# Projections of a hybrid encoder layer as three fp32r products, with the q, k, v stream put first

## The chip, the cores and the metric

The kernel runs on one core of a Trainium2 chip, as one launch. The metric is the device time of that core in microseconds; lower is better. All work of the layer, from reading the inputs in device memory to writing the output there, is in this time.

## The reference

One encoder layer on a sequence of 512 tokens of width 1024 (batch 1), all in float32. The part around the change is the mixer at its start:

```python
h = _rmsnorm(x, norm_mix[l])
u, q, k, v, z, beta_f, beta_b, a_f, a_b = _split_cols(h @ w_in[l])   # w_in: 1024 x 2576
y_s5  = _s5_mixer(u, ...)          # forward and backward complex scan, 32 groups x 64 states
y_gdn = _gdn_mixer(q, k, v, z, beta_f, beta_b, a_f, a_b, ...)
#   depthwise conv of 5 taps + silu on q, k, v; l2norm of q and k;
#   gated delta rule in chunks of 64, forward and backward; times silu(z)
x = x + jnp.concatenate([y_s5, y_gdn], axis=-1) @ w_out[l]
x = x + _mem_xattn(_rmsnorm(x), _rmsnorm(mem), wq, wk, wv, wo)       # 256 memory tokens
x = x + _hier_moe(_rmsnorm(x), ...)                                   # 32 experts, top 2
return _rmsnorm(x, norm_final)
```

u, q, k, v and z are each 512 columns wide, the gates (beta and a, both directions) 16 columns together.

## The kernel before

**Engines and order.** The kernel is written on a layer that takes instructions in program order with a priority, simulates a time line when it is built, and fixes from it one order for each engine's queue. An engine then works through its queue strictly in order: an instruction that waits holds up all behind it. Where several streams are to run beside each other they are Python generators, and `weave` (L44) draws from them in a given proportion; instructions that are ready early can still be moved ahead of others that stand before them in the program.

**Stage one, projections (about 0 to 200 us).** `stage_a` (L154) loads x, normalises it (`rms_T`, L106) and leaves it transposed in the tile `ht` (128 partitions, 8 slices k, 512 tokens, float32): eight slices, TensorE transposes into PSUM, and alternately ScalarE and VectorE bring one slice with its gain back to SBUF (L128 to L131). `proj` (L179) makes 128 columns of `h @ w_in`: the weights come by `wcols` (L134, one DMA of 512 KB on SyncE's queue, tile `wst`, four buffers), and `mm8` (L140) runs eight float32 matmuls of 128x128 weights on 512 tokens. There are 20 such blocks: four of u (`proj_u`, L188), twelve of q, k and v (`gdn_in` and `gdn_conv`, L611 and L627), four of z (`proj_z`, L676). `gates` (L517) makes the 16 columns of the gates with matmuls at L539.

After a q, k or v block the convolution runs: ScalarE copies the block to `xp` (L636) and starts `cv` (L637), VectorE adds four taps (L639), ScalarE applies silu (L640), TensorE transposes (L648), q and k are normalised with a `pow` on GpSimd (L666) and transposed once more (L673). `xp` has two buffers, and its edges are cleared by GpSimd (L633, L634). Beside it runs `s5_params` (L232): a long chain of small VectorE operations, then eight rounds of complex products `cmul` (L221, six tensor products of 128x512 each, on VectorE or GpSimd by the tables at L54 and L55) that make `pm` and `ca`, transposes of `pm` (L372), `s5_u` (L396) and small matmuls (L381). `build` (L1510) weaves the twelve q, k, v blocks with this at L1559.

**Stage two, inverses (about 200 to 285 us).** `gdn_inv` (L685) builds and inverts the triangular blocks. Its tiles are allocated in a pool `gv` (L1563) that takes the place of the tiles of `s5_params`, so they wait until those are done. Beside it run `proj_z`, half of `mem_kv` (L945, keys and values of the memory, float32 matmuls of 256 tokens by the same `mm8`) and the first 16 steps of the recurrence `s5_rec` (L409, four short VectorE operations a step).

**Later stages.** `gdn_chain` (L789) with the rest of `mem_kv` and `s5_rec`, then `s5_out`, `s5_glu`, the mixer's output (`mix`, L920), cross attention and the experts, whose 96 MB of weights stream in as places for them come free. `mix`, `xattn` and `xattn_out` already use `mm3` (L145): a product of two float32 operands as three matmuls in the type fp32r, high times low, high times high and low times high, where the high half is the value copied to fp32r and the low half the rest. The weights of cross attention are split by `wsplit4` (L964): ScalarE copies the high half (L971), GpSimd subtracts (L972).

Of the kernel before, what the change touches and what calls it, by code (L numbers as in the profile page):

```python
# [9 lines left out]
F32 = mybir.dt.float32  # L10
F32R = mybir.dt.float32r
# [3 lines left out]
AF = mybir.ActivationFunctionType  # L15
OP = mybir.AluOpType
# [15 lines left out]
P = 128  # L32
T = 512
# [10 lines left out]
def weave(*streams):  # L44

    live = [[g, n, 0] for g, n in streams]
    while live:
        s = min(live, key=lambda t: (t[2] + 0.5) / t[1])
        s[2] += 1
        if next(s[0], s) is s:  # L50
            live.remove(s)


CA_ENG = (1, 1, 0, 1, 1, 1, 0, 1)  # L54
# [3 lines left out]
class Enc:  # L58
# [44 lines left out]
        return t  # L103


    def rms_T(self, pool, tiles, gain, out, tag, between=None, junk=None):  # L106

        nc = self.nc
        n = len(tiles)
        ss = pool.tile([P, 8], F32, name=tag + "ss", bufs=1)  # L110
        rs = pool.tile([P, 8], F32, name=tag + "rs", bufs=1)
        xn = []
        for i, t in enumerate(tiles):
            sq = junk if junk is not None else pool.tile([P, D], BF16, name=tag + "sq", bufs=1)
            nc.scalar.activation(sq, t, AF.Square, accum_out=ss[:, i:i + 1])
            nc.vector.tensor_scalar(ss[:, i:i + 1], ss[:, i:i + 1], 1.0 / D, 1e-6, op0=OP.mult, op1=OP.add)
            nc.gpsimd.tensor_tensor(rs[:, i:i + 1], ss[:, i:i + 1], self.nhalf[:, 0:1], op=OP.pow)
            nc.vector.tensor_scalar(t, t, rs[:, i:i + 1], None, op0=OP.mult)
            xn.append(t)
        if between:  # L120
            between()
        for k in range(8):
            ps = self.ps("tp")
            for i in range(n):
                nc.tensor.transpose(ps[:, i * P:(i + 1) * P],
                                    xn[i].rearrange("t (p k) -> t k p", k=8)[:, k, :], self.ident)
            src = ps[:, :n * P]
            if k % 2:  # L128
                nc.vector.tensor_scalar(out[:, k, :], src, gain[:, k:k + 1], None, op0=OP.mult)
            else:  # L130
                nc.scalar.activation(out[:, k, :], src, AF.Copy, scale=gain[:, k:k + 1])  # L131
        return xn

    def wcols(self, src, w):  # L134

        t = self.wp.tile([P, 8, w], F32, name="wst", bufs=4)
        self.nc.sync.dma_start(t, src)
        return t

    def mm8(self, ps, w, act):  # L140

# [12 lines left out]
    def stage_a(self):  # L154
        nc, tc, A = self.nc, self.tc, self.A
        pool = self.pa
        gain = self.col8('norm_mix', self.cp)
        x2d = A['x'][0]
        xt = []
        with tc.tile_pool(name="xp", bufs=1) as xp:  # L160
            for i in range(4):
                t = xp.tile([P, D], F32, name=f"x{i}")
                nc.sync.dma_start(t, x2d[i * P:(i + 1) * P, :])
                xt.append(t)
            self.ht = pool.tile([P, 8, T], F32, name="ht")
            self.pre = {}

            def first_weights():
                for c0 in (0, P):
                    self.pre[c0] = self.wcols(self.w_in(c0, P), P)  # L170
                self.w_g = self.wp.tile([P, 8, 16], F32, name="wg", bufs=1)
                nc.sync.dma_start(self.w_g, self.w_in(2560, 16))

            self.rms_T(xp, xt, gain, self.ht, "h", first_weights)

    def w_in(self, c0, w):
        return self.A['w_in'][0].rearrange("(p k) n -> p k n", k=8)[:, :, c0:c0 + w]

    def proj(self, c0):  # L179

        w = self.pre.pop(c0, None)
        if w is None:
            w = self.wcols(self.w_in(c0, P), P)
        ps = self.ps("mm")
        self.mm8(ps, w, self.ht)
        return ps

    def proj_u(self):  # L188
# [328 lines left out]
    def gates(self):  # L517
        nc, A, tc = self.nc, self.A, self.tc
# [5 lines left out]
        with tc.tile_pool(name="gt_", bufs=1) as tp:  # L524
# [6 lines left out]
            ps = self.ps("s5")  # L531
# [2 lines left out]
            sel = tp.tile([P, 16], F32, name="gsel")  # L534
            v.tensor_reduce(sel, self.ident.rearrange("p (i c) -> p c i", i=4)[:, :16], axis=AX.X, op=OP.add)
            for j in range(2):
                for i in range(4):
                    k = j * 4 + i
                    nc.tensor.matmul(ps[i * 32:i * 32 + 16], self.w_g[:, k], self.ht[:, k], start=(j == 0), stop=(j == 1))  # L539
            for i in range(4):  # L540
                nc.scalar.activation(gT[i * 32:i * 32 + 16], ps[i * 32:i * 32 + 16], AF.Copy)
            pt = self.ps("tp")
# [4 lines left out]
            y, ab, e, w, t1 = (tp.tile([P, 4, 8], F32, name="s" + n) for n in "yaewt")  # L547
# [128 lines left out]
    def proj_z(self):  # L676
        nc = self.nc
        for h in range(4):
            ps = self.proj(2048 + h * P)
            z = self.wp.tile([P, T], F32, name="zt", tag="ut", bufs=1)  # L680
            nc.scalar.activation(z, ps, AF.Silu)
            nc.sync.dma_start(self.z_scr[:, h], z)
            yield
# [826 lines left out]
    def build(self):  # L1510
# [41 lines left out]
        with tc.tile_pool(name="gi", bufs=2) as gi:  # L1552
            qkv = self.gdn_in([(w, n, h) for h in range(4) for w, n in ((1, "k"), (0, "q"))] +
                              [(2, "v", h) for h in range(4)], gi)
            s5 = self.s5_params()
            next(s5)
            for _ in u:
                pass
            weave((qkv, 13), (s5, 9))  # L1559

        self.gp2 = pool(left, "gp2")
        self.gp3 = pool(left, "gp3")
# [204 lines left out]
```

## Time and profile before

Three runs took 903.43, 900.66 and 902.88 us (median 902.88). The profile comes from one more execution, which took 903.52 us; its span, from the first to the last instruction, is 901.8 us, so that 1.7 us lie around it.

| what | value |
|---|---|
| TensorE (PE) busy | 790.2 us, 88% of the span, 4735 matmul records |
| TensorE weight loads (PEld) busy | 498.2 us, 55% |
| VectorE (DVE) busy | 406.2 us, 45% |
| ScalarE (ACT) busy | 328.4 us, 36% |
| GpSimd (POOL) busy | 233.9 us, 26% |
| DMA | 185.17 MB, mean 205 GB/s |
| mean granted TensorE clock | 0.942 |

How to read it: a row names the line of the kernel, the engine, the operation, the tile written and the tiles read, shapes, the count, and busy time. A float32 matmul of 512 columns shows as two records of TensorE, an fp32r matmul as one. A busy TensorE need not be at its peak, since matmuls are pipelined and their ends modelled. "Idle before" is time in which the engine waited ahead of these instructions, with the engine or transfer that ended the wait; PEclk is the clock that TensorE was granted, as a share of full speed. Time stamps are microseconds from the span's start.

### The profile page before, as it was taken

The page shows a single profiled execution, that of the slowest core. Times are in us where ns is not written, and L with a number is a line of the kernel's source. Part 1 is how long each engine was busy: PE and PEld are TensorE (multiplying, and loading weights), DVE is VectorE, ACT ScalarE, POOL GpSimd, SP SyncE. Part 2 cuts the span into 40 slices and gives each one's busy share as a digit, 9 for nine tenths or more (in the row PEclk, how much of TensorE's full clock was granted, in tenths as well). Part 3 has the DMA queues.
Part 4 walks back from the last instruction along what each step waited for, and adds up shares of the span by engine and source line. Part 5 has one row for each costly group of instructions (what it writes and reads, how often), then busy time and mean ns, then how long its engine had stood idle before and what let it go on. Part 6 is the DMA issues. An engine that isn't in the chain of part 4 may idle for free. (4 is left out here: it accounts for less than half of the span.)

```text
span 901.8 us, 13009 instructions
## 1 busy us (share of the span) xinstructions
PE 790.2 (88%) x4735; PEld 498.2 (55%) x4736; DVE 406.2 (45%) x1049; ACT 328.4 (36%) x758; POOL 233.9 (26%) x239
## 2 busy tenths in 40 slices
PE   5987998998997997899899999993988888788883
PEld 3444554555686876667688889992333333333331
DVE  4288667878898432245543544216000000000284
ACT  4333444454413355454334554431412221212214
POOL 1032776633100122115161322324111010101203
PEclk9997998999996998999999999996889999999997
DMA  8836222315562337516655324983899999999942
GB/s 208 150 87 100 89 64 73 121 53 187 179 189 60 107 64 175 101 43 205 206 179 182 123 71 164 328 325 123 316 413 413 412 414 412 400 399 407 391 186 95
DMA packets 128130, 185.17 MB, mean 205 GB/s; under 512 B 38734, under 2 KB 93006, under 8 KB 123968
## 3 DMA queue, kind: packets, MB, share of 16 engines
q1 hardware_dynamic: 122736, 172.31, 56.7%
q0 software_dynamic: 5328, 12.01, 3.5%
q8 instruction: 38, 0.62, 0.3%
q14 instruction: 28, 0.23, 0.1%
HBM read 165.50 MB, written 26.18 MB: 213 GB/s over the span
## 5 line engine op out<-in xcount | busy, mean ns | idle before, releaser
L143 PE MATMUL bank<-ht,wst 128*128 128x512 f32 x320 | 152.8, 626 | 2.6 <-ACT kd L583 2.4
L143 PEld LDWEIGHTS bank<-ht,wst 128*128 128x128 f32 x320 | 60.8, 199 | 71.9 <-issue 68.1
L1342 PE MATMUL bank<-mw,xt 128*64 128x512 f32 x320 | 87.7, 607 | 4.1 <-DVE yd L1386 3.3
L1383 PE MATMUL bank<-mw,hT 128*64 128x512 f32 x168 | 54.0, 710 | 19.1 <-ACT hT L1377 19.1
L143 PE MATMUL bank<-mt,wst 128*128 128x256 f32 x256 | 59.7, 392 | 0.0
L1342 PEld LDWEIGHTS bank<-mw,xt 128*64 128x64 f32 x320 | 31.6, 140 | 50.6 <-issue 40.4
L639 DVE SCALAR_TENSOR_TENSOR cv<-xp,taps,cv 128x512 f32<-128x512 f32 x48 | 50.4, 1049 | 20.3 <-ACT cv L637 19.3
L972 POOL TENSOR_TENSOR wlo<-wst,whi 128x1024 fp32r<-128x1024 f32 x16 | 38.6, 2414 | 78.8 <-ACT whi L971 78.8
L1346 DVE SCALAR_TENSOR_TENSOR hs<-hs,tw,bank 128x256 f32<-128x256 f32 x16 | 7.7, 480 | 113.8 <-ACT hs L1345 113.8
L1345 ACT ACTIVATE hs<-bank,tw 128x256 f32<-128x256 f32 x16 | 7.6, 475 | 139.6 <-PE bank L1342 139.6
L143 PEld LDWEIGHTS bank<-mt,wst 128*128 128x128 f32 x256 | 49.9, 198 | 7.7 <-issue 0.8
L1322 POOL DMA_INDIRECT xg<-t_scr,tidx x16 | 16.5, 1033 | 143.8 <-PE bank L1375 128.7
L1386 DVE COPY yd<-bank 128x512 f32<-128x512 f32 x13 | 9.0, 692 | 87.2 <-PE bank L1383 87.2
L824 POOL TENSOR_TENSOR kt<-kn,kd 64x512 f32<-64x512 f32 x14 | 14.5, 1035 | 97.6 <-PE bank L778 51.4
L1383 PEld LDWEIGHTS bank<-mw,hT 128*64 128x64 f32 x168 | 14.8, 158 | 44.3 <-issue 23.3
L1332 ACT ACTIVATE xt<-bank,gm 128x128 f32<-128x128 f32 x128 | 34.8, 383 | 10.2 <-PE bank L1329 10.0
L149 PE MATMUL bank<-wlo,oh 128*128 128x256 f32 x128 | 36.6, 289 | 0.0
L854 DVE SCALAR_TENSOR_TENSOR S<-S,egl,bank 128x128 f32<-128x128 f32 x48 | 15.5, 346 | 46.2 <-PE bank L851 46.2
L150 PE MATMUL bank<-whi,oh 128*128 128x256 f32 x128 | 35.8, 282 | 0.0
L151 PE MATMUL bank<-whi,ol 128*128 128x256 f32 x128 | 35.2, 287 | 0.0
L1342 PE MATMUL bank<-xh,xt 128*64 128x512 f32 x72 | 32.4, 593 | 0.8 <-DVE yd L1386 0.8
L149 PE MATMUL bank<-mlo,mxh 128*128 128x512 f32 x64 | 25.6, 403 | 0.3 <-DVE gss L484 0.3
(556 smaller groups left out, 1853.0 us busy)
## 6 DMA issues: line engine op xcount, KB each, us to landing
mw<-in_moe_w_down_dram SPq DMA_DIRECT2D x25, 1024.0 KB, 13.1
mw<-in_moe_w_gate_dram SPq DMA_DIRECT2D x40, 512.0 KB, 13.7
mw<-in_moe_w_up_dram SPq DMA_DIRECT2D x40, 512.0 KB, 13.3
wst<-in_w_in_dram SPq DMA_DIRECT2D x20, 512.0 KB, 4.5
xh<-in_moe_w_gate_dram SPq DMA_DIRECT2D x9, 512.0 KB, 12.6
xh<-in_moe_w_up_dram SPq DMA_DIRECT2D x9, 512.0 KB, 11.4
ca_scr<-ca SPq DMA_DIRECT2D x8, 512.0 KB, 2.8
wst<-in_xa_wk_dram SPq DMA_DIRECT2D x8, 512.0 KB, 4.5
```

Of the source, the lines that this page charges most:

```text
L143: self.nc.tensor.matmul(ps, w[:, k, :], act[:, k, :], start=(k == 0), stop=(k == 7))
L149: self.nc.tensor.matmul(ps, ah, bl, start=(first and i == 0), stop=False)
L150: self.nc.tensor.matmul(ps, ah, bh, start=False, stop=False)
L151: self.nc.tensor.matmul(ps, al, bh, start=False, stop=(last and i == n - 1))
L639: v.scalar_tensor_tensor(cv, xp[:, w:w + T], taps[:, w, m:m + 1], cv, op0=OP.mult, op1=OP.add)
L824: nc.gpsimd.tensor_tensor(kt[s], self.kn[s, ch // 2], self.kd[s, ch // 2, di * 4:di * 4 + 4, None].to_broadcast([64, 4, P]), op=OP.mult)
L854: v.scalar_tensor_tensor(sn, S[di, h], self.egl[:, ch % 2, ch // 2, di * 4 + h:di * 4 + h + 1], p, op0=OP.mult, op1=OP.add)
L972: nc.gpsimd.tensor_tensor(lo, st, hi.bitcast(F32), op=OP.subtract)
L1322: self.gather = g_.indirect_dma_start(out=xg, out_offset=None, in_=self.t_scr, in_offset=bass.IndirectOffsetOnAxis(ap=self.tidx[:, q:q + 1 ...
L1332: nc.scalar.activation(xt[:, k], ps[:, (k % 4) * P:(k % 4 + 1) * P], AF.Copy, scale=self.gm[:, k:k + 1])
L1342: nc.tensor.matmul(pg[w * 64:w * 64 + 64].rearrange("p (a n) -> p a n", a=2), xt[:, k, w * 64:w * 64 + 64], un[k // 4 * 2 + w][:, :, k % 4 ...
L1383: nc.tensor.matmul(py[w * 64:w * 64 + 64], hT[:, k, w * 64:w * 64 + 64], wd[w][:, k, c], start=(k == 0), stop=(k == 1))
```

## The change

The 20 projection blocks are no longer float32 matmuls but sums of three fp32r products. `ht` becomes two tiles, `hth` and `htl`; `rms_T` with `lo` given writes each slice twice, the high half by ScalarE from PSUM and the low half by VectorE from PSUM. `wsplit` loads a block's weights as before (`wst` has three buffers now), lets ScalarE copy the high half to `whi` and another engine subtract the low half into `wlo` (two buffers each): GpSimd for the first two u blocks and the four z blocks, VectorE for the other two u blocks and the twelve of q, k and v. `proj` calls `mm3` with eight slices: 24 matmuls instead of eight. The gates stay float32 and run twice, on the low and on the high half of h. The stream of the q, k, v blocks is wrapped in `ahead`, which issues all its instructions at high priority, so that the order made at build time prefers them (their loads and splits too) to those of `s5_params` beside them.

```diff
--- before.py
+++ after.py
@@ -49,6 +49,15 @@
         s[2] += 1
         if next(s[0], s) is s:
             live.remove(s)
+
+
+def ahead(tc, g):
+
+    while True:
+        with tc.high_priority():
+            if next(g, g) is g:
+                return
+        yield
 
 
 CA_ENG = (1, 1, 0, 1, 1, 1, 0, 1)
@@ -103,7 +112,7 @@
         return t
 
 
-    def rms_T(self, pool, tiles, gain, out, tag, between=None, junk=None):
+    def rms_T(self, pool, tiles, gain, out, tag, between=None, junk=None, lo=None):
 
         nc = self.nc
         n = len(tiles)
@@ -125,7 +134,11 @@
                 nc.tensor.transpose(ps[:, i * P:(i + 1) * P],
                                     xn[i].rearrange("t (p k) -> t k p", k=8)[:, k, :], self.ident)
             src = ps[:, :n * P]
-            if k % 2:
+            if lo is not None:
+                nc.scalar.activation(out[:, k, :], src, AF.Copy, scale=gain[:, k:k + 1])
+                nc.vector.scalar_tensor_tensor(lo[:, k, :], src, gain[:, k:k + 1], out[:, k, :].bitcast(F32),
+                                               op0=OP.mult, op1=OP.subtract)
+            elif k % 2:
                 nc.vector.tensor_scalar(out[:, k, :], src, gain[:, k:k + 1], None, op0=OP.mult)
             else:
                 nc.scalar.activation(out[:, k, :], src, AF.Copy, scale=gain[:, k:k + 1])
@@ -133,9 +146,18 @@
 
     def wcols(self, src, w):
 
-        t = self.wp.tile([P, 8, w], F32, name="wst", bufs=4)
+        t = self.wp.tile([P, 8, w], F32, name="wst", bufs=3)
         self.nc.sync.dma_start(t, src)
         return t
+
+    def wsplit(self, src, w, lo_eng):
+
+        st = self.wcols(src, w)
+        hi = self.wp.tile([P, 8, w], F32R, name="whi", bufs=2)
+        lo = self.wp.tile([P, 8, w], F32R, name="wlo", bufs=2)
+        self.nc.scalar.activation(hi, st, AF.Copy)
+        lo_eng.tensor_tensor(lo, st, hi.bitcast(F32), op=OP.subtract)
+        return hi, lo
 
     def mm8(self, ps, w, act):
 
@@ -162,27 +184,26 @@
                 t = xp.tile([P, D], F32, name=f"x{i}")
                 nc.sync.dma_start(t, x2d[i * P:(i + 1) * P, :])
                 xt.append(t)
-            self.ht = pool.tile([P, 8, T], F32, name="ht")
+            self.hth = pool.tile([P, 8, T], F32R, name="hth")
+            self.htl = pool.tile([P, 8, T], F32R, name="htl")
             self.pre = {}
 
             def first_weights():
                 for c0 in (0, P):
-                    self.pre[c0] = self.wcols(self.w_in(c0, P), P)
+                    self.pre[c0] = self.wsplit(self.w_in(c0, P), P, nc.gpsimd)
                 self.w_g = self.wp.tile([P, 8, 16], F32, name="wg", bufs=1)
                 nc.sync.dma_start(self.w_g, self.w_in(2560, 16))
 
-            self.rms_T(xp, xt, gain, self.ht, "h", first_weights)
+            self.rms_T(xp, xt, gain, self.hth, "h", first_weights, lo=self.htl)
 
     def w_in(self, c0, w):
         return self.A['w_in'][0].rearrange("(p k) n -> p k n", k=8)[:, :, c0:c0 + w]
 
-    def proj(self, c0):
-
-        w = self.pre.pop(c0, None)
-        if w is None:
-            w = self.wcols(self.w_in(c0, P), P)
+    def proj(self, c0, lo_eng=None):
+
+        hi, lo = self.pre.pop(c0, None) or self.wsplit(self.w_in(c0, P), P, lo_eng or self.nc.vector)
         ps = self.ps("mm")
-        self.mm8(ps, w, self.ht)
+        self.mm3(ps, [((hi[:, k, :], lo[:, k, :]), (self.hth[:, k, :], self.htl[:, k, :])) for k in range(8)])
         return ps
 
     def proj_u(self):
@@ -534,9 +555,11 @@
             sel = tp.tile([P, 16], F32, name="gsel")
             v.tensor_reduce(sel, self.ident.rearrange("p (i c) -> p c i", i=4)[:, :16], axis=AX.X, op=OP.add)
             for j in range(2):
-                for i in range(4):
-                    k = j * 4 + i
-                    nc.tensor.matmul(ps[i * 32:i * 32 + 16], self.w_g[:, k], self.ht[:, k], start=(j == 0), stop=(j == 1))
+                for part in (self.htl, self.hth):
+                    for i in range(4):
+                        k = j * 4 + i
+                        nc.tensor.matmul(ps[i * 32:i * 32 + 16], self.w_g[:, k], part[:, k].bitcast(F32),
+                                         start=(j == 0 and part is self.htl), stop=(j == 1 and part is self.hth))
             for i in range(4):
                 nc.scalar.activation(gT[i * 32:i * 32 + 16], ps[i * 32:i * 32 + 16], AF.Copy)
             pt = self.ps("tp")
@@ -676,7 +699,7 @@
     def proj_z(self):
         nc = self.nc
         for h in range(4):
-            ps = self.proj(2048 + h * P)
+            ps = self.proj(2048 + h * P, nc.gpsimd)
             z = self.wp.tile([P, T], F32, name="zt", tag="ut", bufs=1)
             nc.scalar.activation(z, ps, AF.Silu)
             nc.sync.dma_start(self.z_scr[:, h], z)
@@ -1556,7 +1579,7 @@
             next(s5)
             for _ in u:
                 pass
-            weave((qkv, 13), (s5, 9))
+            weave((ahead(tc, qkv), 13), (s5, 9))
 
         self.gp2 = pool(left, "gp2")
         self.gp3 = pool(left, "gp3")
```

## The prediction

> **What bounds the kernel now.** I read the page first, then a table of all engines by stage, the matmuls of L143 by stage, the waits of the second stretch, and the time line around single operations.
>
> ```profile
> PE 790.2 (88%) x4735; PEld 498.2 (55%) x4736; DVE 406.2 (45%) x1049; ACT 328.4 (36%) x758; POOL 233.9 (26%) x239
> ```
>
> 88% is a mean over unlike stages, so it says little. The table by stage (TensorE, weight loads, VectorE, ScalarE, GpSimd, then granted clock, DMA share, GB/s):
>
> ```profile
> 0.00:60.00 60.00, 49.53 (x163) 24.77 (x164) 29.82 (x141) 24.61 (x44) 6.48 (x15) 1.00 0.70 156
> 60.00:200.00 140.00, 127.12 (x834) 67.53 (x835) 103.79 (x150) 61.68 (x173) 82.68 (x86) 0.93 0.34 85
> 200.00:245.00 45.00, 42.54 (x345) 25.03 (x344) 39.02 (x147) 21.75 (x27) 10.38 (x6) 0.96 0.49 169
> 245.00:285.00 40.00, 34.06 (x251) 30.41 (x250) 39.41 (x173) 9.20 (x19) 0.00 (x0) 0.91 0.52 154
> 590.00:902.00 312.00, 245.83 (x1208) 114.51 (x1207) 68.53 (x160) 77.23 (x226) 54.77 (x60) 0.91 0.85 335
> ```
>
> The change works in the first three rows. From 60 to 200 us TensorE is busy 127 of 140 us, but VectorE is busy 104 and GpSimd 83: no engine has much room. From 200 to 285 us VectorE is the full one (78 of 85 us). The experts at the end move 335 GB/s, and their loads go out as places for them come free, so time saved ahead of them should reach the end whole.
>
> How much of this is the projections (the same stages, L143 alone: TensorE, weight loads):
>
> ```profile
> 0.00:60.00 60.00, 37.59 (x80) 15.10 (x80) 1.00 0.70 156
> 60.00:200.00 140.00, 86.44 (x176) 33.89 (x176) 0.93 0.34 85
> ```
>
> A block is 16 records, so five blocks lie before 60 us and eleven between 60 and 200; the four of z follow. What VectorE, GpSimd and TensorE wait for in that second stretch:
>
> ```profile
> POOL xp L633 <- DVE cv L639: 21.4, 7, 6.4
> DVE cv L639 <- ACT cv L637: 19.3, 8, 4.2
> ...
> PE bank L372 <- DVE pm L228: 5.7, 1, 5.7
> ```
>
> The convolution waits 19.3 us for ScalarE's copy, which waits for the projection. GpSimd stands 21.4 us before its clearing of `xp`, because the convolution still holds that buffer. This is a ring through TensorE, ScalarE, VectorE and GpSimd; TensorE is its longest part, VectorE the next.
>
> **The change part by part.** *TensorE.* Twenty float32 records in a row and the instruction behind them; two fp32r matmuls of 512 columns, 29 steps apart; the gates:
>
> ```profile
> 125.80 8.85 PE L143 MATMUL bank<-ht,wst 128*128 128x512 f32 x20
> 134.58 1.03 PE L404 MATMUL bank<-uperm,bct 128*64 128x64 f32 x28
> ...
> 465.37 0.39 PE L149 MATMUL bank<-mlo,mxh 128*128 128x512 f32 x1
> ...
> 471.94 0.39 PE L149 MATMUL bank<-mlo,mxh 128*128 128x512 f32 x1
> ...
> 28.03 1.91 PE L539 MATMUL bank<-ht,wg 128*16 128x512 f32 x16
> ```
>
> A float32 record takes (134.58 − 125.80)/20 = 0.439 us, a block of 16 records 7.0 us. An fp32r matmul takes (471.94 − 465.37)/29 = 0.227 us, a block of 24 takes 5.4 us. A block saves 1.6 us of TensorE: 8 us in the first five, 17.5 in the eleven, 6.4 in z, 32 in all. The gates run twice: +1.9. So TensorE loses 30 us of work, and that is the ceiling of the gain.
>
> *What comes in elsewhere.* Attention does the same operations already: ScalarE's high half of 128x1024, VectorE's low half of it, the pair that brings a slice from PSUM, and GpSimd's low half (least, median and greatest ns):
>
> ```profile
> L1001 ACT ACTIVATE kvh<-kvs x4: 1050/1060/1063, 496.4 to 506.2; 128x1024 fp32r<-128x1024 f32 x4
> L1002 DVE TENSOR_TENSOR kvl<-kvs,kvh x4: 1208/1224/2592, 497.5 to 507.3; 128x1024 fp32r<-128x1024 f32 x4
> L985 ACT ACTIVATE xh<-bank,c_norm_xattn x8: 682/691/703, 474.2 to 489.4; 128x512 fp32r<-128x512 f32 x8
> L986 DVE SCALAR_TENSOR_TENSOR xl<-bank,c_norm_xattn,xh x8: 742/743/751, 474.9 to 490.4; 128x512 fp32r<-128x512 f32 x8
> L972 POOL TENSOR_TENSOR wlo<-wst,whi x16: 2378/2398/2665, 463.9 to 596.7; 128x1024 fp32r<-128x1024 f32 x16
> ```
>
> Twenty high halves are 20 x 1.06 = 21 us of ScalarE, 12 of them between 60 and 200 us. It is busy 108 of the first 245 us, so they lie beside other work; without that room each would add its 1.06 us to a block. Fourteen low halves go to VectorE, at 1.21 us alone and 2.59 at worst, and six to GpSimd at 2.40. The slices cost four more operations of 0.69 us on ScalarE and four more of 0.74 on VectorE.
>
> *Why 2.59.* VectorE and GpSimd hold each other up. Here are four taps of a convolution beside GpSimd's products, two taps without them, and a product of the recurrence of 64 columns that meets one GpSimd operation, with the mean of its like:
>
> ```profile
> 123.22 5.45 DVE L639 SCALAR_TENSOR_TENSOR cv<-xp,taps,cv 128x512 f32<-128x512 f32 x4 [3.42 <-ACT cv L637]
> 75.17 1.53 DVE L639 SCALAR_TENSOR_TENSOR cv<-xp,taps,cv 128x512 f32<-128x512 f32 x2
> 222.43 1.26 DVE L414 TENSOR_TENSOR rt<-a8r,U 128x64 f32<-128x64 f32 x1
> 222.35 1.26 POOL L725 TENSOR_TENSOR qkd<-qkd,mk 128x512 f32<-128x512 f32 x1 [4.24 <-DVE qkd L724]
> L416 DVE TENSOR_TENSOR rt<-rt,rt 128x64 f32<-128x64 f32 x49 | 10.9, 222 | 0.8
> ```
>
> A tap takes 0.77 us alone and 1.36 in company, and the short product takes 1.26 us instead of 0.22 and ends just behind GpSimd's. The Trainium skill ("SBUF — State Buffer", section "SBUF: two separate sides") says that GpSimd and a VectorE operation with two SBUF inputs take one shared port pair in turns, each for its whole instruction. The trace agrees in these rows. By that rule alone, every low half would add its whole time to the other engine's queue, and the time would come out as in the rival "lock" below.
>
> *The second stretch, 60 to 200 us.* TensorE falls from 127.1 to 109.6 us. VectorE takes in eleven low halves; between 1.21 and 2.59 I take the middle, 1.9, since GpSimd is busy in 83 of the 140 us: +21, so 125 us. VectorE becomes the fullest engine, and it has waits of its own. The fullest engine now runs at 127/140 = 91%; at 93 to 95% for VectorE the stretch takes 131 to 134 us. I take a gain of 7. With 1.21 us a half VectorE has 117 us and at 93% the stretch takes 126: gain 14. With 2.59 it has 132 us, at 93% 142: loss of 2.
>
> *Priority.* The q, k, v stream now passes the products of `s5_params` on VectorE and GpSimd, and their stores on SyncE's queue: its loads, splits, taps and clearings go first. TensorE's wait of 5.7 us for `pm` goes, as the first convolution no longer stands behind those products and projections fill the hole. But `s5_params` ends later, and the inverses wait for its tiles. Today both end together; these are its last small matmuls and the first of the inverses:
>
> ```profile
> 195.94 0.66 PE L381 MATMUL bank<-ca,bb 64*32 64x128 f32 x16
> ...
> 200.60 0.68 PE L703 MATMUL bank<-lef,g 128*64 128x64 f32 x16
> ```
>
> I bound this by the size of that hole both ways, −6 to +6, and take −2, as z and the memory's keys can fill TensorE during a tail of `s5_params`.
>
> *The first 60 us.* TensorE alone doesn't set this stage:
>
> ```profile
> ACT ut L194 <- DMA u_scr<-ut: 6.2, 1, 6.2
> ...
> DVE fq L214 <- ACT ft L213: 6.4, 1, 6.4
> ```
>
> ScalarE waits 6.2 us with the second u block for the store of the first (`ut` has one buffer), and everything behind it on ScalarE waits too, so the chain of `s5_params` on VectorE stands 6.4 us. A quicker TensorE starts the store sooner but doesn't shorten it. At best the five blocks give 8; at worst the first block waits for its two halves (1.06 + 2.40) and the gates' 1.9 come on top, some 5 lost. I take a gain of 3.
>
> *After 200 us.* z gives TensorE 6.4 us, but VectorE is the full engine. GpSimd's four low halves can stop VectorE for 2.40 each: 0 to +9.6. In return the memory's blocks start sooner, and one of them stands between two matmul groups of the inverse:
>
> ```profile
> 278.78 6.82 PE L768 MATMUL bank<-XT,N 32*32 32x32 f32 x128 [5.94 <-issue]
> ...
> 286.01 6.22 PE L143 MATMUL bank<-mt,wst 128*128 128x256 f32 x16
> ```
>
> Moved into the hole of 5.94 us ahead, it gives up to 6. So −6 to +10; I take −1, since the recurrence, which fills much of VectorE here, can partly wait.
>
> *The sum.* −7 − 2 − 3 − 1 = −13 against the profiled execution's 903.5 us: 890.5. The median of the runs shown is 0.6 under that execution, so 890.
>
> **The rivals.** *Lock* (slower). VectorE and GpSimd become one resource. The second stretch loses 2, the four halves of z stop the inverses for 9.6, the first stage gives its 3: +8.6, so 911 us. For it: 1.36 against 0.77 us a tap. Against: GpSimd idles 57 of 140 us there, and z's halves may be made before the inverses begin. It decides once VectorE's mean low half is above 2.2 us.
>
> *Tail* (no change). q, k and v finish sooner, but `s5_params`, now behind them, ends at 200 us as before, since its work on GpSimd isn't less; the inverses start when they did. The first stage's 3 are lost in it, and some 3 remain from after 200 us: 900 us. For it: both streams end together today. Against: 21.4 us of GpSimd's waits hang on the convolution and shrink with it. If the priority alters no order at all, only its 2 us are missing.
>
> *Through* (much faster). TensorE's ring is the true bound everywhere, and all 30 us come through: 873 us. For it: 91% busy, and VectorE's largest wait (19.3 us) hangs on a projection. Against: VectorE's load above. The Trainium skill ("TensorE: Matmul & The Clock Gate", Part 1) adds that idle windows halve the clock, which a less filled TensorE would meet more often; by it this rival would end some us higher.
>
> **How the numbers follow.** Forecast 0.45, *through* 0.20, *lock* 0.20, *tail* 0.15. The forecast's own range is 878 to 902. To leave no more than 2 in 10 out, the range reaches from *through* to near *lock*: 873 to 909. A measurement of this kernel can tell about 0.3% (2.7 us) from no change. Faster by more than that: 0.43 of the forecast, all of *through*, a third of *tail*: 0.68. Within it: half of *tail* and the edges: 0.11. Slower: *lock* and the rest: 0.21.
>
> **What would show it.** In the profile after, L150 and its neighbours should show 24 records a block, 0.227 us apart; the low halves on VectorE a mean near 1.9 us; the first L703 near 188 us instead of 200.60; VectorE fuller than TensorE up to there. The forecast is wrong if L703 starts at 200 us or later, if the low halves come near 2.6 us, or if TensorE still is the fullest and the inverses start before 180 us.

## The result and the profile after

The changed kernel takes 899.07 us (median of 20 runs, 887.6 to 904.05); the kernel before takes 901.69 beside it (20 runs, 899.17 to 905.27). The ratio of the compared runs is 0.9931, with a 95% interval of 0.9910 to 0.9951: about 6 us faster. The comparisons here leave out runs more than 1.5% above the fastest of their kernel: five of these twenty (the other fifteen have a median of 896.31 us), two of the six of split_ut2_tz2 below, which stood near 1117 us at a granted clock of 0.64, and one of the kernel before at 2643 us. By the medians of all twenty runs on each side the change is only 2.6 us faster, so its worth is 3 to 6 us by the way of counting. The profiled execution of the changed kernel took 900.03 us, its span 898.2.

The first lines of the page, the table by stage (columns as before) and the matmuls that open the inverses, all of the changed kernel:

```profile
PE 779.6 (87%) x4911; PEld 539.8 (60%) x4912; DVE 434.9 (48%) x1067; ACT 348.6 (39%) x781; POOL 256.6 (29%) x245
```

```profile
0.00:60.00 60.00, 45.48 (x215) 33.80 (x217) 33.66 (x151) 34.61 (x59) 10.19 (x17) 0.94 0.71 157
60.00:200.00 140.00, 121.73 (x1009) 92.92 (x1008) 124.66 (x161) 73.01 (x182) 98.06 (x88) 0.93 0.38 93
200.00:245.00 45.00, 37.75 (x325) 31.06 (x325) 41.74 (x131) 21.32 (x28) 14.35 (x8) 0.96 0.46 161
245.00:285.00 40.00, 37.16 (x379) 32.67 (x378) 34.71 (x155) 12.03 (x24) 1.20 (x2) 0.91 0.44 127
```

```profile
L726 PE MATMUL bank<-lef,g x64: 222/222/270, 193.8 to 221.5; 128*64 128x64 f32 x64
```

TensorE's busy time fell by 10.6 us in all, not by 30. VectorE is now the fullest engine from 60 to 200 us, with the 125 us that were forecast. The inverses open at 193.8 instead of 200.60 us, where the prediction had 188. The waits of that stretch, one row of the kernel before that the prediction doesn't show, then those of the changed kernel:

```profile
ACT cv L640 <- DVE cv L639: 46.0, 10, 8.7
```

```profile
ACT cv L663 <- DVE cv L662: 25.0, 6, 8.0
POOL xp L656 <- DVE cv L662: 18.4, 6, 6.6
...
PE bank L393 <- DVE pm L249: 3.8, 2, 3.0
...
DVE cv L662 <- ACT cv L660: 1.9, 3, 1.1
```

Before, VectorE's taps waited 19.3 us for ScalarE's copy of a projection. Now they wait 1.9: the projections are ready when VectorE comes to them. ScalarE's wait for the taps is no sign of this, as it went down too, from 46.0 to 25.0 us.

The recurrent chain of the delta rule opens with the first `vn`. In the kernel before, then in the changed one (the two times are the first and the last start):

```profile
L841 ACT ACTIVATE vn<-bank,csv x32: 338/367/379, 300.4 to 415.9; 128x128 f32<-128x128 f32 x32
```

```profile
L864 ACT ACTIVATE vn<-bank,csv x32: 362/368/380, 284.9 to 405.3; 128x128 f32<-128x128 f32 x32
```

At 285 us the change is 15.5 us ahead, more than the whole forecast. At the last addition of the S5 half to the residual (481.4 instead of 482.8 us) 1.4 are left. What lies between is seen in the table for 340 to 412 us of the changed kernel:

```profile
340.00:364.00 24.00, 21.83 (x192) 16.40 (x190) 6.96 (x21) 15.31 (x27) 4.93 (x12) 0.93 0.71 138
364.00:388.00 24.00, 23.78 (x124) 18.15 (x124) 5.88 (x13) 4.67 (x10) 0.43 (x4) 0.51 0.07 26
388.00:412.00 24.00, 23.61 (x198) 18.09 (x196) 11.83 (x25) 12.10 (x27) 3.08 (x8) 1.00 0.32 104
```

TensorE looks full in the middle row, but its granted clock is 0.51, and it gets 124 matmuls done where the next row has 198. Ahead of this stands one gap, in the time line of TensorE:

```profile
362.09 0.38 PE L825 MATMUL bank<-vn,qkd 64*64 64x128 f32 x2
364.22 0.66 PE L467 MATMUL bank<-tz,uperm 128*64 128x128 f32 x2 [1.75 <-issue]
```

L467 is the first product of the second half of `s5_out`, and it needs the second load of `tz`. That tile has one buffer, so SyncE issues the load's eight pieces once the first half's products are done, and each takes 7.2 us to land (time line of SyncE, then the view of the tile):

```profile
353.29 3.76 SPq L451 DMA_DIRECT2D tz<-w_scr  x8
```

```profile
DMA to landing us min/median/max: 7.0/7.2/7.4
```

The last piece is issued at 356.6 and lands near 363.8 us; TensorE starts at 364.22. The row names no transfer ("issue"), so that this load is the cause is shown only by the run below that takes the wait away. The runs' own clocks say the same: at a mean granted clock of 0.941 the changed kernel took 889.07 us, at 0.928 it took 897.14 to 900.03, and at 0.924 it took 900.16 to 904.05. Not every run fits (one took 899.01 at 0.934).

### The profile page after: what moved, and what is told of

It is laid out like the page before. It is cut to its first block, busy times and chain, and to the rows that moved or that the text cites. A ratio compares the mean times of both kernels' runs of the same rounds, so it can differ in the third digit from the quotient of the medians.

```text
span 898.2 us, 13385 instructions
## 1 busy us (share of the span) xinstructions
PE 779.6 (87%) x4911; PEld 539.8 (60%) x4912; DVE 434.9 (48%) x1067; ACT 348.6 (39%) x781; POOL 256.6 (29%) x245
## 3 DMA queue, kind: packets, MB, share of 16 engines
q1 hardware_dynamic: 122736, 172.31, 57.4%
## 5 line engine op out<-in xcount | busy, mean ns | idle before, releaser
L171 PE MATMUL bank<-htl,whi 128*128 128x512 f32 x160 | 68.0, 426 | 5.0 <-ACT ut L215 1.9
L165 PE MATMUL bank<-mt,wst 128*128 128x256 f32 x256 | 62.8, 405 | 4.6 <-ACT zt L704 4.6
L172 PE MATMUL bank<-hth,whi 128*128 128x512 f32 x160 | 65.6, 410 | 0.0
L1406 PE MATMUL bank<-mw,hT 128*64 128x512 f32 x168 | 48.9, 665 | 19.2 <-ACT hT L1400 19.2
L173 PE MATMUL bank<-hth,wlo 128*128 128x512 f32 x160 | 65.3, 409 | 0.0
L165 PEld LDWEIGHTS bank<-mt,wst 128*128 128x128 f32 x256 | 51.3, 204 | 13.1 <-ACT zt L704 5.0
L662 DVE SCALAR_TENSOR_TENSOR cv<-xp,taps,cv 128x512 f32<-128x512 f32 x48 | 47.4, 989 | 2.3 <-ACT cv L660 1.9
L847 POOL TENSOR_TENSOR kt<-kn,kd 64x512 f32<-64x512 f32 x14 | 14.5, 1036 | 93.4 <-PE bank L801 48.6
L171 PEld LDWEIGHTS bank<-htl,whi 128*128 128x128 f32 x160 | 32.1, 201 | 14.5 <-ACT ut L215 2.4
L1406 PEld LDWEIGHTS bank<-mw,hT 128*64 128x64 f32 x168 | 13.8, 150 | 41.9 <-ACT hT L1400 21.1
L1355 ACT ACTIVATE xt<-bank,gm 128x128 f32<-128x128 f32 x128 | 34.8, 383 | 10.3 <-PE bank L1352 10.2
L173 PEld LDWEIGHTS bank<-hth,wlo 128*128 128x128 f32 x160 | 31.7, 198 | 7.2 <-DVE wlo L159 0.4
L877 DVE SCALAR_TENSOR_TENSOR S<-S,egl,bank 128x128 f32<-128x128 f32 x48 | 15.7, 346 | 42.0 <-PE bank L874 41.9
```

The lines of the kernel that those rows point to most:

```text
L165: self.nc.tensor.matmul(ps, w[:, k, :], act[:, k, :], start=(k == 0), stop=(k == 7))
L171: self.nc.tensor.matmul(ps, ah, bl, start=(first and i == 0), stop=False)
L172: self.nc.tensor.matmul(ps, ah, bh, start=False, stop=False)
L173: self.nc.tensor.matmul(ps, al, bh, start=False, stop=(last and i == n - 1))
L662: v.scalar_tensor_tensor(cv, xp[:, w:w + T], taps[:, w, m:m + 1], cv, op0=OP.mult, op1=OP.add)
L847: nc.gpsimd.tensor_tensor(kt[s], self.kn[s, ch // 2], self.kd[s, ch // 2, di * 4:di * 4 + 4, None].to_broadcast([64, 4, P]), op=OP.mult)
```

## The experiments

Theory after the result: the early gain is real, and some 12 us of it are lost to half clock (24 us at half speed) behind the wait for `tz`. Rival: the order of work in `s5_out` and `s5_glu` changed, and the clock is a bystander. Beside that stood the prediction's own terms. The table collects times and points of the profiled executions (us): the end of the gates, the first matmul of the inverses, the first `vn`, the last product of `s5_out` (L467 and its like), and the last addition of the S5 half. The clock is that of the profiled execution.

| kernel | median | clock | gates | inverses | chain | s5_out | S5 added |
|---|---|---|---|---|---|---|---|
| before | 901.7 | 0.942 | 61.2 | 200.6 | 300.4 | 387.7 | 482.8 |
| changed | 899.07 | 0.928 | 57.1 | 193.8 | 284.9 | 392.7 | 481.4 |
| split_only | 889.52 | 0.937 | 58.2 | 194.2 | 291.1 | 378.6 | 471.3 |
| priority_only | 898.18 | 0.943 | 75.7 | 223.5 | 298.8 | 378.8 | 474.1 |
| after_tz2 | 889.37 | 0.937 | 57.4 | 194.1 | 285.2 | 378.2 | 469.7 |
| before_tz2 | 900.05 | 0.939 | 61.6 | 200.7 | 300.5 | 384.7 | 480.2 |
| split_tz2 | 889.62 | 0.937 | 58.5 | 193.4 | 287.9 | 373.4 | 470.9 |
| ut2_tz2 | 886.45 | 0.938 | 52.7 | 189.2 | 282.8 | 372.7 | 463.8 |
| before_ut2_tz2 | 888.98 | 0.944 | 54.1 | 190.4 | 289.9 | 373.7 | 470.0 |
| split_ut2_tz2 | 888.4 | 0.935 | 55.2 | 191.8 | 289.4 | 374.4 | 471.3 |
| z_dve_tz2 | 885.49 | 0.940 | 57.0 | 195.9 | 283.7 | 367.4 | 465.1 |
| lo_pool_tz2 | 913.85 | 0.924 | 58.9 | 224.2 | 313.6 | 397.9 | 495.3 |
| no_wlo_tz2 | 1113.72 | 0.853 | 67.1 | 181.1 | 280.3 | 363.0 | 459.7 |
| two_prod_tz2 | 875.66 | 0.919 | 59.9 | 181.6 | 268.1 | 364.0 | 457.1 |

**Where the early gain went.** One edit, in both kernels:

```diff
-                tzh = sp.tile([P, 16, 8, 16], F32, name="tz", bufs=1)
+                tzh = sp.tile([P, 16, 8, 16], F32, name="tz", bufs=2)
```

> The changed kernel with two buffers for the tile tz of s5_out instead of one, so that the second half's load does not wait for the first half's products. Theory (clock): what the change won by the start of the chain (15.5 us) was lost again because a wait of 1.75 us for this load put TensorE to half clock for 24 us, from 364 to 388 us. Without that wait the half clock from 285 to 430 us is under 12 us in all (34 in the changed kernel), the chain ends near 394 instead of 405 us, and the time is 887 to 893, with less spread from run to run. Rival (order): the loss comes from the order of work in that stage, with the recurrence 8 us later and glu behind the chain; then the wait goes but the time stays within 3 us of the changed kernel's 899.

> The kernel before with two buffers for tz, the control of the other. In its profile the wait for this load is 3.25 us, with 3.4 us at half clock behind it, so about 5 us. Theory (clock): 3 to 6 us of gain, 896 to 899, much less than the 10 that the same edit gives the changed kernel. Rival (order): 2 us or less.

The changed kernel falls to 889.37 us (884.69 to 890.99; ratio to before 0.9829, interval 0.9789 to 0.9869), 9.7 below the median of all runs of the changed kernel and 6.9 below that of the fifteen compared. The kernel before falls to 900.05 (ratio 0.9969, 0.9943 to 0.9994), 2 us where 3 to 6 were expected, which is the number of that run's rival. The same 24 us of after_tz2 as above:

```profile
364.00:388.00 24.00, 24.00 (x223) 18.71 (x224) 11.48 (x29) 13.05 (x28) 1.46 (x5) 1.00 0.17 58
```

There are 223 matmuls at a clock of 1.00 instead of 124 at 0.51. Up to the chain's start the two kernels agree within 0.3 us, so the 14.5 us at the end of `s5_out` are the wait and its clock: 1.75 of gap and half of 24. Two numbers missed: the chain's last `vn` starts at 397.2 us where 394 was expected, and the clock over 285 to 430 us is 0.93, some 20 us at half speed, where under 12 was expected; some 14 of them lie between 330 and 360 us (granted clocks 0.65, 0.84 and 0.83 in three slices of 10 us), ahead of the place that the edit touches. For the changed kernel the theory holds and the rival falls (it allowed 3 us of change); that the same wait costs the kernel before as much as its gap and 3.4 us at half clock is not shown.

**The two parts apart.** The one without `ahead`, the other the kernel before with `ahead` alone:

```diff
-            weave((ahead(tc, qkv), 13), (s5, 9))
+            weave((qkv, 13), (s5, 9))
```

> The change without its priority: q, k, v projections are products of halves, but stand in the two streams' own order. The prediction's parts: priority was worth 2 us, so the start of the chain (300.4 us before, 284.9 after) should come near 287, and the time 1 to 3 us above that of the whole change. Rival: the priority makes most of the early gain, because the halves' splits otherwise queue behind the products of s5_params; then the chain starts at 293 us or later and the time is 5 us or more above that of the whole change.

> The kernel before with the priority alone, all products in float32. The prediction's part: 2 us of gain at the start of the chain (298 us), within 3 us of 901 in time. Rival, priority makes most of the early gain: the chain starts at 293 us or sooner. Second rival: TensorE is the fullest engine here, so the priority only puts s5_params later; inverses start later than 204.8 us and the time is 2 to 6 us longer.

> The change without its priority, with two buffers for tz. Beside the changed kernel with two buffers for tz (889.4 us; first matmul of the inverses 194.1, chain from 285.2) it prices the priority with the wait for tz out of the way. Theory (priority is worth about 2 us here, as predicted): 889 to 893, and the chain starts 2 to 6 us later. Rival (the priority only reorders, and the chain's earlier start is given back before the end): within 2 us of 889.4 either way, though the chain starts some 6 us later.

The split alone gives 889.52 us (ratio 0.9836, 0.9796 to 0.9877): 7 to 10 less than the whole change (by its two medians), though its chain starts 6 us later. Neither of its theories expected that. Its order of work meets half clock for a shorter time in `s5_out` (last product 378.6 us). With the wait for `tz` out of the way the two are equal, 889.62 and 889.37. So the priority's earlier chain is given back before the S5 half is added (470.9 and 469.7 us), as the rival had it.

The priority alone gives 0.9944 (0.9922 to 0.9966), 5 us rather than 2, by a way that none of its theories had: the gates end at 75.7 and the inverses open at 223.5 us, much later, as its second rival had it, yet the chain starts at 298.8. The q, k, v blocks move ahead, TensorE then stands 13 us for the first `pm` of `s5_params`, and more of the recurrence runs beside the chain (some 39 of its 62 steps lie ahead of the chain, 55 in the kernel before):

```profile
72.54 1.94 PE L381 MATMUL bank<-ident,pm 128*128 128x128 f32 x8 [13.08 <-DVE pm L237]
```

**What sets 60 to 200 us.** Two kernels leave work out. The first makes no low halves of the weights, and its third product takes the high half again; the second also leaves out that product, an estimated 36 us of TensorE (160 matmuls of 0.227 us). Cuts of the two edits, the second below the dots:

```diff
-        lo = self.wp.tile([P, 8, w], F32R, name="wlo", bufs=2)
         self.nc.scalar.activation(hi, st, AF.Copy)
-        lo_eng.tensor_tensor(lo, st, hi.bitcast(F32), op=OP.subtract)
-        return hi, lo
+        return hi, hi
...
-        self.mm3(ps, [((hi[:, k, :], lo[:, k, :]), (self.hth[:, k, :], self.htl[:, k, :])) for k in range(8)])
+        for k in range(8):
+            self.nc.tensor.matmul(ps, hi[:, k, :], self.htl[:, k, :], start=(k == 0), stop=False)
+            self.nc.tensor.matmul(ps, hi[:, k, :], self.hth[:, k, :], start=False, stop=(k == 7))
```

> The changed kernel with two buffers for tz; the low halves of the weights of u, q, k, v and z are left out, and the third product takes the high half again. TensorE keeps its 24 matmuls a block; VectorE loses fourteen operations (20 us) and GpSimd six (14 us). Theory (VectorE is the fullest engine from 60 to 200 us, as predicted): the first matmul of the inverses comes at 182 to 188 instead of 194.1 us, the chain starts near 276 instead of 285, the time is 878 to 884. Rival (TensorE's ring still bounds that stretch): the inverses start at 191 us or later and the time is within 3 us of 889.4.

> As the kernel without the low halves of the weights, and without the third product too: a block is 16 fp32r matmuls. TensorE loses a third of every block, 20 x 1.8 = 36 us, of it some 20 between 60 and 200; VectorE and GpSimd are as in that kernel. With wrong values the experts at the end take another path, so only the times up to the end of attention count. Theory (VectorE with its waits sets the stretch from 60 to 200 us): the first matmul of the inverses within 5 us of that kernel's 181.1. Rival (TensorE's ring sets it): 170 us or sooner.

Without the low halves the inverses open at 181.1 instead of 194.1 us, although the gates end 10 us later, and the S5 half is added 10.0 us sooner. Of this kernel only the points before the experts count: the third product with the high half again changes the values, the experts do other work (4961 matmul records in all instead of 4911), and the 1113.72 us compare with nothing. The chain starts at 280.3, later than the 276 expected. Taking a third of every block off TensorE as well leaves the inverses where they are (181.6), brings the chain to 268.1, and the S5 half only 2.6 us further. This one was run once; its 4751 matmul records are those of after_tz2 without the 160 left out, so its 875.66 us can be compared, 13.7 below. The second stretch by the table of stages, of no_wlo_tz2 and of two_prod_tz2:

```profile
60.00:200.00 140.00, 126.41 (x1086) 98.94 (x1085) 113.68 (x192) 81.13 (x194) 87.71 (x88) 0.91 0.39 95
```

```profile
60.00:200.00 140.00, 110.86 (x987) 83.75 (x988) 116.20 (x183) 77.72 (x189) 90.62 (x88) 0.84 0.38 91
```

TensorE is busy 15 us less and the inverses start no sooner. VectorE and GpSimd set their start: the 34 us of low halves in all (20 and 14) were worth 13 us at the inverses and 10 at the S5 half, TensorE's 36 us nothing at the inverses, 12.2 at the chain and 2.6 at the S5 half. What TensorE gives up is thus seen behind the inverses only, and most of it is gone again at the S5 half; why was not looked into.

**Which engine takes the low halves.** All on GpSimd, or z's on VectorE:

```diff
-        hi, lo = self.pre.pop(c0, None) or self.wsplit(self.w_in(c0, P), P, lo_eng or self.nc.vector)
+        hi, lo = self.pre.pop(c0, None) or self.wsplit(self.w_in(c0, P), P, self.nc.gpsimd)
```

```diff
-            ps = self.proj(2048 + h * P, nc.gpsimd)
+            ps = self.proj(2048 + h * P)
```

> The changed kernel with two buffers for tz and all twenty low halves of the weights on GpSimd. VectorE loses 16 us between 60 and 200, GpSimd takes in eleven more operations of 2.4 us, 26 us. Rival of the prediction (lock, one resource for both): what the two do together grows by 11 x 1.2 = 13 us, the first matmul of the inverses comes at 200 us or later, and the time is 893 or more. Theory of the prediction (VectorE alone is the fullest, GpSimd has room): the inverses start at 193 us or sooner and the time is 889 or less.

> The changed kernel with two buffers for tz and z's four low halves on VectorE (1.22 us each) instead of GpSimd (2.4). The prediction put 0 to 9.6 us on GpSimd's halves stopping VectorE during the inverses. If they do stop it: the last inverse block (229.8 us) and the chain's start (285.2) come 2 to 5 us sooner. If they fall into time in which VectorE waits anyway: VectorE gains 5 us of work, and these come 0 to 5 us later. Time 886 to 894 in both cases.

With all low halves on GpSimd the time is 913.85 us, 24.5 worse. The direction is that of *lock*, the size twice its 13. A likely reason, not tested by itself, is that GpSimd also makes 54 of the 96 products of `s5_params` in that stretch, in order, and that TensorE waits for one of them:

```profile
PE bank L393 <- POOL P L246: 15.9, 1, 15.9
```

z's four halves moved the other way bring the last inverse block 4.7 us forward and the chain's start 1.5. These are the blocks' first VectorE operations, in after_tz2 and then in z_dve_tz2:

```profile
L730 DVE TENSOR_TENSOR e<-bank,gc x4: 679/682/693, 201.0 to 229.8; 128x512 f32<-128x512 f32 x4
```

```profile
L730 DVE TENSOR_TENSOR e<-bank,gc x4: 682/685/692, 200.6 to 225.1; 128x512 f32<-128x512 f32 x4
```

GpSimd's halves do stop VectorE. In after_tz2 a product of the recurrence, 0.22 us by itself, takes 2.44 and ends just behind such a half:

```profile
217.44 2.40 POOL L159 TENSOR_TENSOR wlo<-wst,whi 128x1024 fp32r<-128x1024 f32 x1
217.49 2.44 DVE L436 TENSOR_TENSOR rt<-a8i,U 128x64 f32<-128x64 f32 x1
```

With one more of 1.23 us beside the other half of that time this is some 3 us, an estimate, and VectorE takes two halves of 1.22 us in their place. So the stops alone don't make the 4.7: TensorE, which stood 3.5 us between 200 and 230 us, stands no more (30.0 of 30 us busy instead of 26.5). At 885.49 us (881.84 to 886.22) this is the lowest median of the kernels that leave nothing out, 0.9813 of before (0.9771 to 0.9855).

**The wait that the prediction had named.** Two buffers for `ut` (and for `zt`, which shares its place), beside two for `tz`:

```diff
-            u = self.wp.tile([P, 8, 64], F32, name="ut", tag="ut", bufs=1)
+            u = self.wp.tile([P, 8, 64], F32, name="ut", tag="ut", bufs=2)
```

> The changed kernel with two buffers for tz, and two for ut, so that the second u block's copy does not wait for the first one's store. In the changed kernel ScalarE waits 4.5 us for that store, TensorE stands 1.6 us at 50 us and runs at half clock around it. Theory (this wait holds up the first 60 us, as predicted): the end of the gates comes 2 to 4 us sooner than 57.4, the granted clock up to 60 us is 1.00 instead of 0.94, and the time is 884 to 887. Rival (the loads of x and the chain of s5_params set this stage): the gates end within 1 us of 57.4 and the time is within 2 us of 889.4.

> The kernel before with two buffers for ut and for tz: the change's control with both waits out of the way. Beside the changed kernel with the same two (886.4) it gives the change's own worth. Theory: what the change wins early is 15 us at the chain's start, of which 10 to 13 reach the end when no clock is lost on the way: 896 to 899. Rival (the gain came from these waits rather than from the products): 892 or less.

> The change without its priority, with two buffers for ut and for tz: the candidate for the fastest version. If the priority is worth nothing with the waits out of the way: within 2 us of 886.4. If it gives 2 us, as predicted: 888 to 890. If it costs: 884 or less.

In the changed kernel the gates end 4.7 us sooner, the clock up to 60 us is 1.00 as expected, and the time is 886.45 us (884.37 to 888.62; 0.9844, 0.9817 to 0.9870). In the kernel before, all float32, the same edits give 888.98 us (885.03 to 893.12; 0.9862, 0.9824 to 0.9899): 12 us, of which 2 were `tz`'s. My theory had 896 to 899, and its rival is right: most of what the change won is to be had without it, from the wait for `ut`'s store. The second buffer of `zt` has no part in the early gain: the inverses open 10.3 us sooner (190.4 instead of 200.7) before the first `zt` is written (200.5 us). The second stretch of before_ut2_tz2:

```profile
60.00:200.00 140.00, 131.45 (x925) 71.31 (x923) 102.32 (x159) 65.25 (x176) 77.55 (x79) 0.94 0.35 86
```

Here TensorE is 94% busy, fuller than in any other kernel of the table from 60 to 200 us, and the products of halves should help most. Yet beside the changed kernel with both edits the inverses come 1.2 us and the chain 7.1 us later, and the medians are 2.5 us apart with intervals that overlap. With `ut` waiting the change was worth 10.7 us (900.05 to 889.37), without it 2.5 by the medians and 5.7 between the two profiled executions (890.11 and 884.37). The priority is worth 2 in this pair, by a median of 888.4 for split_ut2_tz2 whose spread of 885 to 892.5 takes in the 886.45.

## Why the prediction was right, and where it was not

The forecast was faster, by 13 us to 890; it became 6 by the runs compared and 2.6 by the medians of all. The range of 873 to 909 held, but it is wide, and 899 is rather the number of *tail* (900) than the forecast's. The terms of the sum did not come out as written, and none of the three rivals came by its own mechanism.

**TensorE's 30 us.** A matmul step at full clock is 0.227 us as taken, and a block is 24 of them:

```profile
145.78 0.50 PE L171 MATMUL bank<-htl,whi 128*128 128x512 f32 x1
...
151.13 0.39 PE L173 MATMUL bank<-hth,wlo 128*128 128x512 f32 x1
151.45 0.63 PE L402 MATMUL bank<-ca,bb 64*32 64x128 f32 x6
```

That block took 5.7 us. Others met half clock, where a step is 0.43 us (53.44 less 53.01, in the first stage, where the mean clock fell from 1.00 to 0.94):

```profile
53.01 0.63 PE L173 MATMUL bank<-hth,wlo 128*128 128x512 f32 x1
53.44 0.63 PE L171 MATMUL bank<-htl,whi 128*128 128x512 f32 x1
```

With `tz`'s wait gone on both sides, TensorE is busy 15 us less, half of the 30 (before_tz2, then after_tz2):

```profile
PE 787.8 (88%) x4735; PEld 497.0 (55%) x4736; DVE 406.8 (45%) x1049; ACT 328.9 (37%) x758; POOL 233.1 (26%) x239
```

```profile
PE 772.5 (87%) x4911; PEld 533.8 (60%) x4912; DVE 434.3 (49%) x1067; ACT 348.8 (39%) x781; POOL 256.5 (29%) x245
```

**First 60 us: −3 forecast, −4.1 measured** (gates 61.2 to 57.1). The reading that ScalarE's wait for the store of `ut` holds this stage was right, and ut2_tz2 shows it. What I didn't do is price that row for itself: 6.2 us of one engine, worth 10 us at the inverses. Nor did a quicker TensorE start the store sooner. In the kernel before the copy into `ut` ends at 33.6 us, but the store stands in SyncE's queue behind other loads until 37.4 and lands near 41.9:

```profile
28.76 6.15 SPq L609 DMA_DIRECT2D taps<-in_gdn_conv_dram  x5
35.02 2.25 SPq L137 DMA_DIRECT2D wst<-in_w_in_dram  x1
37.38 0.59 SPq L195 DMA_DIRECT2D u_scr<-ut  x1
```

In the changed kernel it goes out at 38.4 us. So 3.8 of the 6.2 us are the order of that queue; issuing the store first was not tried.

**Second stretch with the priority: −9 forecast, −2.7 measured.** From the gates to the inverses it was 139.4 us and is 136.7. This is the step that failed. Its sum of 125 us for VectorE came true, by another route. The eleven low halves took 16.2 us instead of the 21 given them (1.47 each, not 1.9), but the 42 products of `s5_params` on VectorE slowed from 37.1 to 45.8 us in all, with GpSimd busy 98 us beside them instead of 83. The low halves of the changed kernel (VectorE, GpSimd); then the product that grew most, in the kernel before and in the changed one:

```profile
60.00:200.00 140.00, 16.18 (x11) 4.94 (x2) 0.93 0.38 93
```

```profile
L228 DVE TENSOR_TENSOR pm<-pm,P 128x512 f32<-128x512 f32 x5 | 3.4, 685 | 0.0
```

```profile
L249 DVE TENSOR_TENSOR pm<-pm,P 128x512 f32<-128x512 f32 x5 | 6.5, 1300 | 0.0
```

The mis-sized term is how full VectorE can be: I took 93 to 95% for the fullest engine and it reached 89% (121.4 of the 136.7 us from the gates to the inverses). 125/0.89 is 140, so nearly all of the gain of 7 was gone. VectorE's waits in that stretch sum to 14.6 us, where the prediction left it 6 to 9. The longest are for ScalarE's high halves and for the small products of `s5_params` on TensorE:

```profile
DVE wlo L159 <- ACT whi L158: 4.1, 3, 2.2
DVE wl L409 <- PE bank L402: 3.2, 1, 3.2
DVE wl L408 <- PE bank L402: 2.9, 1, 2.9
```

That VectorE, with GpSimd, and not TensorE sets the stretch was right, as no_wlo_tz2 and two_prod_tz2 show; so *through* fell. That GpSimd had room there was wrong, as lo_pool_tz2 shows.

**After 200 us: −1 forecast, −8.7 measured** (from the first inverse matmul to the chain 99.8 us before, 91.1 after). The reason given, that the recurrence can partly wait, is seen in the trace: of its 62 steps 55 lay ahead of the chain's start, and now 41 do. These are the last operations of the steps up to there (L417 in the kernel before, L438 in the changed one):

```profile
200.00:300.40 100.40, 12.55 (x55) 0.92 0.46 148
```

```profile
200.00:284.90 84.90, 9.97 (x41) 0.94 0.45 145
```

So part of the 8.7 us is work that was put off, not work that is gone. How much of the 8.7 it makes was not tested.

The cost given to GpSimd's halves was real too; z_dve_tz2 puts it at 4.7 us at the last inverse block and 1.5 at the chain. The Trainium skill ("SBUF — State Buffer", section "SBUF: two separate sides") has GpSimd and a VectorE operation with two SBUF inputs take turns at one port pair. This agrees with 685 against 1300 ns above, with the 2.44 us beside z's half and with the direction of lo_pool_tz2.

**The end whole.** Time saved ahead of the experts did reach the end: after_tz2 is 13.1 us ahead when the S5 half is added, and 12.8 at the end of the profiled execution. But I took everything between 285 and 480 us as given, and there the change lost 14 of its 15.5 us. The prediction had no term for a stage that it doesn't touch, and it weighed idle windows and half clock beside *through* alone. The forecast of 890 agrees with after_tz2's 889.4, but two errors of some 6 and 8 us cancel in that, which is luck.

**The rivals.** *Lock* was to decide above 2.2 us a low half; the mean is 1.47 in the stretch. *Tail* had the inverses where they were, and they came 6.8 us sooner. The price of 2 for the priority can't be told from nothing: 0 in one pair, 2 in another, 5 alone, and 7 to 10 lost with the clock.

What stays open: why the gains of the split and of `ut`'s second buffer don't add, since the chain still starts 7 us sooner (with both buffers, too, 41 steps of the recurrence lie ahead of it in the changed kernel and 54 in the kernel before, so that start is in part work put off); and what the order with z on VectorE and both extra buffers together would take, which was not run.

## What to carry to other kernels

Price the longest wait that the profile shows at a buffer with one place before making the work around it cheaper: here a second buffer of 2 KB a partition gave what twenty rewritten projections gave (888.98 against 889.37 us, both with two buffers for `tz`), and most of the two gains is the same gain. Work taken off a full engine is worth what the next one leaves, and two engines that slow each other down may not get as full as one can: here VectorE reached 89%, TensorE before it 91 to 94%. Follow an early gain through the stages that the change doesn't touch, down to short gaps on TensorE, and compare the mean granted clock of runs before explaining a spread.

## What the runs showed of the hardware

A gap of 1.75 us was followed by 24 us at half clock, without another gap (23.78 of 24 us busy). In the kernel before, a gap of 3.25 us at the same load was followed by about 3.4 us of it:

```profile
369.28 0.40 PE L446 MATMUL bank<-tz,uperm 128*64 128x128 f32 x2 [3.25 <-DMA tz<-w_scr]
```

```profile
364.00:388.00 24.00, 20.71 (x184) 15.90 (x185) 7.21 (x20) 9.04 (x19) 2.49 (x6) 0.93 0.39 84
```

The Trainium skill ("TensorE: Matmul & The Clock Gate", Part 1) gives full clock back after one busy window of some 3.4 us. The kernel before agrees with that and the changed kernel differs: TensorE, busy by the profile, did not regain full clock for seven such windows. The matmuls of that stretch are float32, move 128 columns each and have a weight load each, but those behind the gap of the kernel before are of the same lines and shapes, so their size alone is not the reason; it stays open. The spread of the changed kernel's times, 887.6 to 904 us, goes largely with this clock (0.941 to 0.923), and one wait taken away narrows it to 884.7 to 891.0, in six runs.
